# Moving the operand tiles of TensorE to other byte offsets in a hybrid decoder layer

## The chip, the cores and the metric

The kernel runs on one core of a Trainium2 chip. The metric is device time in microseconds of one execution. Four compute engines matter: TensorE (PE in the profile, with its weight loads as a row of their own, PEld), VectorE (DVE), ScalarE (ACT) and GpSimd (POOL). SyncE (SP) issues most of the transfers. A product on PE has a stationary operand of 128 rows by 128 columns, which a weight load brings into the array, and a moving operand of 128 rows by up to 512 columns that streams through it. Both are read from the on-chip memory (SBUF), where a tile occupies the same byte range in each of 128 partitions; an address below is a byte offset in a partition.

## The reference

One layer over 512 tokens of width 1024, all in float32: a norm, one wide input projection, two token mixers side by side, a gated merge with a residual, and an MLP with a residual and a last norm.

```python
h = rms_norm(x, norm_mix[l])
proj = h @ w_in[l]
u, q, kc, vc, ksl, vsl, kwn, vwn, g_nsa, g_merge = jnp.split(proj, IN_SPLITS, axis=-1)
y_pool = pool_mixer(u, w_pool[l], pool_scale[l])
y_nsa = nsa_mixer(q, kc, vc, ksl, vsl, kwn, vwn, g_nsa, ...)
g_a, g_b = jnp.split(jax.nn.sigmoid(g_merge), 2, axis=-1)
merged = g_a * (y_pool @ w_proj_pool[l]) + g_b * (y_nsa @ w_proj_nsa[l])
x = x + merged @ w_out[l]
h = rms_norm(x, norm_mlp[l])
x = x + jnp.square(jax.nn.relu(h @ w_ff1[l])) @ w_ff2[l]
return rms_norm(x, norm_final)
```

The pooling mixer takes causal means over windows of 2, 4, 8 and 16 tokens. The other mixer is attention with 16 heads of 64 over compressed keys, selected blocks and a window; with 512 tokens all blocks are selected and the window holds all tokens.

## The kernel before

Each float32 product is made of three products in the fp32r type: operand A is split into a high part AH and a low part AL, B likewise, and AH·BH, AH·BL and AL·BH are summed in PSUM (`split_products`). ScalarE makes the high part of a weight by a copy, VectorE the low part by a subtraction. So every operand of PE exists as a pair of tiles.

The work goes in stages, in the order of the program, which is written out by hand:

- Tokens are loaded, normed, turned and split into `hT = (R1, R2)`, two tiles of 128 partitions by 8 blocks by 512 tokens. (0 to about 30 us.)
- The input projection: for each key of the list `P1` the 128 columns of weights are loaded into one of four `raw` buffers, split into a slot `wh`, `wl` (two slots of each), and multiplied with `hT` by `fm`: 8 blocks by 3 products of 512 columns with the weights stationary. The first two keys and the second half of the gates (`Group`, keys with G) run at 256 columns instead.
- The attention loop: 96 steps, each with scores, exponentials, transposes and products with the values, and beside them as filler the keys of `FILL2`, again 512-column products of `hT` with `wh`, `wl`. Its result goes into `OT`, which is `hT` again.
- The projections `pn0` to `pn7` of `OT`, the merge, and `w_out`, partly by seven sums of 256 columns (`Out`), partly at 512 columns with resident tiles `mH`, `mL` and `W1H`, `W1L`.
- The MLP, four chunks. Both layers use Strassen-like sums of seven products for four. Layer 1 (`Group`) multiplies weights that stand still with token tiles of 256 columns: `x11`, `x21`, `x22`, `xT1` live in quarters of R1 and R2 (`Rf`, `XB`), `xT2`, `xT3`, `xT4` in the pool `a4`. Its results become `y` tiles (`YB`). Layer 2 of the first three chunks (`Wide`) holds the `y` tiles stationary and streams 512 columns of weights; the last chunk does it at 256 columns (`Out`) and the rest at 512 or 256 (`last_half`).

In the MLP and around it a weight goes into one of three slots in turn: two of `wh`, `wl` and one of `w3h`, `w3l`, which is put ahead in the list `slots_hl`. `product` and `Wide.pe` issue the products in the order that their loops give, and every 6 or 3 products the next step of a weight's preparation and of the side work.

Tiles come from pools. A pool lays its tiles one behind another in the order in which they are first asked for, each start rounded up to 32 bytes; pools stand behind each other in the order of opening, and a closed pool's room is used again. The pool `const` holds `ident`, `eps_t`, R1, R2, MA, `tick`, GB (also `scratch` and a tile `TS` of sums) and `identR`; behind it stand `weights` (`raw`, `wh`, `wl`), then the pools of the stages: `op` and `att` with `p0`, `p1`, `p2` in turn, later `p3` (x1, `sq`), `p4` (`w3h`, `w3l`, `raw5`, `junk`), and above them `q3` and, after it, `a4`.

Of the kernel before, what the change touches and what calls it, by code (L numbers as in the profile page):

```python
# [13 lines left out]
F32 = mybir.dt.float32  # L14
FR = mybir.dt.float32r
# [5 lines left out]
S = 512  # L21
# [4 lines left out]
NT = S // 128  # L26
# [36 lines left out]
def trunk(ctx: ExitStack, tc: tile.TileContext, A, out):  # L63
# [4 lines left out]
    def pool(name, **kw):  # L68
        return tc.tile_pool(name=name, bufs=1, reuse_waits="tile", **kw)
# [8 lines left out]
    cp = ctx.enter_context(pool("const"))  # L78
    wp = ctx.enter_context(pool("weights"))

    ident = cp.tile([128, 128], F32, name="ident")
    eps_t = cp.tile([128, 1], F32, name="eps_t")
    R1 = cp.tile([128, 8, S], FR, name="R1")
    R2 = cp.tile([128, 8, S], FR, name="R2")
    MA = cp.tile([128, 8, S], F32, name="MA")
    MAf = MA.rearrange("p j t -> p (j t)")

# [3 lines left out]
    def quarter(f, i):  # L91
        return f[:, 1024 * i:1024 * i + 1024].rearrange("p (k t) -> p k t", k=4)
# [510 lines left out]

    hT = (R1, R2)
    f_banks = [2]
# [43 lines left out]
    def bcast(v, n):  # L649
        return bass.AP(tensor=v.tensor, offset=v.offset, ap=[[0, 128], [1, n]])  # L650

    POOL.memset(eps_t, EPS)
    tick = cp.tile([128, 1], F32, name="tick")
    ACT.activation(tick, eps_t, AF.Sqrt)
    e2 = ExitStack()
    op = e2.enter_context(pool("op"))
# [190 lines left out]
    with ExitStack() as c1:  # L847
# [247 lines left out]
        for k in P1[2:]:  # L1095
            i = int(k[-1]) if k[-1].isdigit() else None
            if k[-2] == "G":
                if not gate_f:
                    t = p1.tile([128, 16, 128], FR, tag="cA", bufs=1, name="gs")
# [47 lines left out]
    with ExitStack() as c2:  # L1147
# [237 lines left out]
        n = len(slots)  # L1385
# [4 lines left out]
        for i in range(n + LAG + PLAG):  # L1390
            if i < n:
                p = slots[i][0]
# [9 lines left out]
            t = i - LAG  # L1402
# [19 lines left out]
            j = t - PLAG  # L1422
# [26 lines left out]
    p3 = ctx.enter_context(pool("p3"))  # L1449
    ps3 = ctx.enter_context(pool("ps3", space=PSUM))  # L1450
    XX = p3.tile([128, NT, D], F32, name="x1")
    X1 = [XX[:, t, :] for t in range(NT)]
    sq = p3.tile([128, NT, 8], F32, name="sq")

    def bank():
        return ps3.tile([128, S], F32, tag="B", bufs=8, name="psB")
# [8 lines left out]
    def tm3_resident(ws, aT, post):  # L1465

        for t in range(NT):
            ps = bank()
            prods = []
            for k in range(8):  # L1470
                wH, wL = ws[k // 2]
                prods += split_products(*aT(k, t), wH[:, k % 2, :], wL[:, k % 2, :])
            for _ in pieces(ps, prods, prepare=t > 0):
                step_side()
            post(t, ps)
# [6 lines left out]
    XQ = {b: quarter(MAf, i) for i, b in enumerate(("11", "12", "21", "22"))}  # L1482
    XT = quarter(GBf, 0)
    turned = [0]
    Rf = [R.rearrange("p j t -> p (j t)") for R in (R1, R2)]
    XB = {b: [quarter(f, i) for f in Rf] for i, b in enumerate(("11", "21", "22", "T1"))}
    slots_hl.insert(0, [p4.tile([128, 1024], FR, name=f"w3{e}") for e in "hl"])
    give_back(p4.tile([128, 1024], F32, name="raw5"))
# [119 lines left out]
    with ExitStack() as c3:  # L1608
        q3 = c3.enter_context(pool("q3"))
        gB = q3.tile([128, D], F32, name="gB1")  # L1610
        nc.sync.dma_start(gB, bcast(A["norm_mlp"][0], D))
        mT = (q3.tile([128, 8, S], FR, name="mH"), q3.tile([128, 8, S], FR, name="mL"))
        W1 = (q3.tile([128, 8, S], FR, name="W1H"), q3.tile([128, 8, S], FR, name="W1L"))
        keep([f"wo1{i}" for i in range(4)], W1)
# [13 lines left out]
        class Merged:  # L1628
# [4 lines left out]
            def of(self, y):  # L1633
                return self.made[y]
# [24 lines left out]
        for j in range(3, 8):  # L1659
# [10 lines left out]
            if j == 3:  # L1670
                x, y = (M.part(b, slice(0, 4)) for b in ("11", "12"))
# [71 lines left out]
            side.append(g)  # L1743
        tm3_resident(w1, mTs, post1)
    a4 = ctx.enter_context(pool("a4"))
    for b in ("T2", "T3", "T4"):
        XB[b] = [a4.tile([128, 4, 256], FR, name=f"x{b}{e}") for e in "HL"]

    YB = {b: [a4.tile([128, 4, 256], FR, name=f"y{b}{e}") for e in "HL"]
          for b in ("11", "21", "22", "T1", "T2", "T3", "T4")}  # L1750
    YF = {"11": quarter(GBf, 0), "12": quarter(GBf, 1), "21": quarter(GBf, 2), "22": quarter(MAf, 1)}

    def halves(x, f):
# [2 lines left out]
    class Hidden:  # L1756
# [10 lines left out]
        def of(self, b):  # L1767
            return XB["T2"] if b == "12" else YB[b]

# [188 lines left out]
```

## Time and profile before

| | |
|---|---|
| median of 3 runs | 792.78 us (792.71 to 793.98) |
| the profiled execution | 792.2 us, span 790.4 us |
| busy: PE, PEld | 774.8 us, 685.7 us |
| busy: DVE, ACT, POOL | 658.6 us, 504.6 us, 175.1 us |
| products | 4795 |
| granted clock | 0.999 |
| DMA | 140.80 MB, mean 178 GB/s |

The span is from the first to the last instruction of the program; the device time has a little before and after it. A row of a group of instructions has its line, engine, operation, the tile that it writes and those that it reads (buffer numbers left out, so R1 and R2 are both R, and `wh` is either of two slots), the shape and the count; behind the bar the time in which any of the group ran, the mean duration of one in ns, and the idle time before them. Products overlap: the next one starts before the one before has ended, so durations do not add up. The timeline has the start of each instruction and its duration in us; equal ones in succession are merged into one row with their count.

### The profile page before, as it was taken

How to read it: one execution, taken by the hardware profiler on the slowest of the kernel's cores; microseconds unless marked ns; L12 is line 12 of the kernel's file. 1: busy time of each engine (PE TensorE's matmuls, PEld its weight loads, DVE VectorE, ACT ScalarE, POOL GpSimd, SP SyncE). 2: the span in 40 equal slices, each digit the busy share in tenths (PEclk: the TensorE clock that was granted, in tenths of full speed). 3: DMA queues.
4: the chain of work that ended last, by engine and by line, in shares of the span. 5: the costliest groups of instructions: out<-in, count | busy, mean ns of one | idle time of the engine just before them, and what ended most of it. 6: DMA issues, size and time to landing. Idle time of an engine off the chain costs nothing. (4 is left out here: it accounts for less than half of the span.)

```text
span 790.4 us, 13452 instructions
## 1 busy us (share of the span) xinstructions
PE 774.8 (98%) x4795; PEld 685.7 (87%) x4795; DVE 658.6 (83%) x1274; ACT 504.6 (64%) x977; POOL 175.1 (22%) x257
## 2 busy tenths in 40 slices
PE   8999999999999999999999999999999999999996
PEld 6889889878878888888889899879987999799986
DVE  6999858557989988998689689997899789998974
ACT  6668536337978888899545576943783378347833
POOL 4000000015847766563000210101110110010001
PEclk9999999999999999999999999999999999999999
DMA  9453732474566731011667998979998999897622
GB/s 302 129 163 99 196 94 83 118 212 121 74 160 115 162 67 41 27 55 60 165 208 211 294 228 250 289 200 292 288 280 215 297 270 287 213 267 217 189 78 107
DMA packets 118013, 140.80 MB, mean 178 GB/s; under 512 B 5477, under 2 KB 94729, under 8 KB 117770
## 3 DMA queue, kind: packets, MB, share of 16 engines
q1 hardware_dynamic: 98026, 116.64, 45.8%
q0 software_dynamic: 19632, 22.55, 19.1%
q8 instruction: 38, 0.62, 0.3%
q10 hardware_dynamic: 288, 0.75, 0.3%
q14 instruction: 29, 0.24, 0.1%
HBM read 135.20 MB, written 47.19 MB: 231 GB/s over the span
## 5 line engine op out<-in xcount | busy, mean ns | idle before, releaser
L497 PE MATMUL psF<-R,wh 128*128 128x512 f32 x448 | 145.9, 403 | 0.8 <-ACT scratch L869 0.8
L349 ACT ACTIVATE wh<-raw 128x1024 fp32r<-128x1024 f32 x70 | 73.8, 1056 | 72.3 <-PE psB L567 28.5
L311 POOL DMA_DIRECT2D S<-w_ff x40 | 45.1, 1128 | 311.2 <-DMA S<-w_ff 202.9
L352 DVE TENSOR_TENSOR wl<-raw,wh 128x1024 fp32r<-128x1024 f32 x70 | 85.2, 1220 | 18.9 <-ACT wh L349 18.6
L1316 POOL TENSOR_SCALAR P<-P,sm,GT 128x128 f32<-128x128 f32 (+3 forms) x128 | 85.2, 684 | 69.8 <-DVE sm L1313 44.6
L497 PEld LDWEIGHTS psF<-R,wh 128*128 128x128 f32 x448 | 80.5, 188 | 15.8 <-ACT scratch L869 1.0
L497 PE MATMUL psF<-R,wl 128*128 128x512 f32 x224 | 89.1, 398 | 1.3 <-DVE wl L456 1.3
L454 ACT ACTIVATE wh<-raw 128x512 fp32r<-128x512 f32 (+1 forms) x84 | 49.9, 618 | 58.9 <-PE psF L497 31.0
L1303 ACT ACTIVATE P<-P,sm 128x128 f32<-128x128 f32 (+3 forms) x128 | 71.1, 557 | 8.8 <-DVE sm L1293 6.0
L456 DVE TENSOR_TENSOR wl<-raw,wh 128x512 fp32r<-128x512 f32 (+1 forms) x82 | 56.4, 702 | 22.6 <-ACT wh L454 22.2
L1293 DVE CUSTOM_DVE_ANT_0 P<-psS,cst 128x128 f32<-128x128 f32 (+3 forms) x128 | 59.4, 482 | 4.8 <-PE psT L1333 2.4
L567 PE MATMUL psB<-R,wh 128*128 128x256 f32 x336 | 60.8, 282 | 0.0
L1349 DVE TENSOR_TENSOR PT<-psT,PT 128x512 fp32r<-128x512 f32 (+2 forms) x96 | 56.2, 591 | 3.4 <-ACT PT L1344 3.0
L349 ACT ACTIVATE w3h<-raw 128x1024 fp32r<-128x1024 f32 x35 | 37.0, 1057 | 33.5 <-PE psB L567 14.3
L1344 ACT ACTIVATE PT<-psT 128x512 fp32r<-128x512 f32 (+2 forms) x96 | 49.2, 521 | 12.2 <-PE psT L1333 10.9
L567 PEld LDWEIGHTS psB<-R,wh 128*128 128x128 f32 x336 | 51.7, 189 | 0.4
L497 PEld LDWEIGHTS psF<-R,wl 128*128 128x128 f32 x224 | 42.1, 188 | 11.1 <-DVE wl L456 1.8
L1333 PE MATMUL psT<-ident,P 128*128 128x128 f32 x320 | 50.1, 272 | 0.2
L1367 PE MATMUL psO<-PT,VV 128*128 128x256 f32 x320 | 48.5, 286 | 0.0
L352 DVE TENSOR_TENSOR w3l<-raw,w3h 128x1024 fp32r<-128x1024 f32 x35 | 42.7, 1219 | 6.3 <-ACT w3h L349 6.2
L1333 PEld LDWEIGHTS psT<-ident,P 128*128 128x128 f32 x320 | 39.7, 140 | 8.8 <-issue 1.2
L567 PE MATMUL psB<-R,wl 128*128 128x256 f32 x168 | 47.2, 281 | 0.0
(487 smaller groups left out, 2215.2 us busy)
## 6 DMA issues: line engine op xcount, KB each, us to landing
raw<-w_ff SPq DMA_DIRECT2D x55, 512.0 KB, 6.9
S<-w_ff POOLq DMA_DIRECT2D x40, 512.0 KB, 8.6
raw<-S SPq DMA_DIRECT2D x40, 512.0 KB, 5.3
raw<-w_in SPq DMA_DIRECT2D x32, 512.0 KB, 4.1
S<-w_ff SPq DMA_DIRECT2D x30, 512.0 KB, 7.4
S<-S SPq DMA_DIRECT2D x10, 512.0 KB, 6.4
raw<-w_proj_nsa SPq DMA_DIRECT2D x8, 512.0 KB, 3.9
x<-x SPq DMA_DIRECT2D x7, 512.0 KB, 6.5
```

The costliest lines, as they stand in the source:

```text
L349: ACT.activation(h, t, AF.Copy)
L352: DVE.tensor_tensor(l, t, h.bitcast(F32), op=ALU.subtract)
L454: ACT.activation(h[:, sl], t[:, sl], AF.Copy)
L456: eng.tensor_tensor(l[:, sl], t[:, sl], h[:, sl].bitcast(F32), op=ALU.subtract)
L497: PE.matmul(ps, a, b, start=first and j == 0, stop=last and j == n - 1, skip_group_check=True)
L567: PE.matmul(out, w[u][:, k, 128 * f:128 * f + 128], moving[v][:, k, :], **kw)
L1293: DVE.tensor_tensor_reduce(out=P[:, o:o + n].rearrange("p (a c) -> p a c", c=128), in0=s, in1=m, scale=1.0, scalar=3e38, op0=ALU.add, op1= ...
L1303: last_exp[:] = [ACT.activation(c, c, AF.Exp, bias=sm[:, 0, e:e + 1], scale=-1.0, accum_out=sm[:, 1, e:e + 1])]
L1316: r = POOL.tensor_scalar(P[:, o:o + n], P[:, o:o + n], sm[:, 2, e:e + 1], GT[:, qb, c + e:c + e + 1], op0=ALU.mult, op1=ALU.mult)
L1333: PE.transpose(pt[:, 128 * j:128 * j + 128], P[:, 128 * j:128 * j + 128], ident)
L1344: ACT.activation(dH, src, AF.Copy)
L1349: return DVE.tensor_tensor(dL, src, dH.bitcast(F32), op=ALU.subtract)
```

## The change

The tiles get other addresses, by five edits; no instruction is added, removed or put elsewhere, apart from the operands' addresses.

- `tick` is asked for ahead of R1 instead of behind MA.
- R1 and R2 become 64 and 8 elements longer, and each has two views: the plain one, from element 0, in 8 blocks, for `hT` and `OT`; and a flat one from element 8 (32 bytes on), which takes the place of `Rf` in the quarters of the MLP and of `w_out`.
- An unused tile of 56 elements stands ahead of the weights' tiles, another ahead of `mH`.
- `sq` has 16 elements a token block instead of 8.
- In `a4` the `y` tiles come first, then an unused tile of 8 elements, then the `x` tiles.

```diff
--- before.py
+++ after.py
@@ -80,8 +80,16 @@
 
     ident = cp.tile([128, 128], F32, name="ident")
     eps_t = cp.tile([128, 1], F32, name="eps_t")
-    R1 = cp.tile([128, 8, S], FR, name="R1")
-    R2 = cp.tile([128, 8, S], FR, name="R2")
+    tick = cp.tile([128, 1], F32, name="tick")
+
+    def two_bases(name, n):
+
+        t = cp.tile([128, n], FR, name=name)
+        return t[:, 0:8 * S].rearrange("p (j t) -> p j t", j=8), t[:, 8:8 + 8 * S]
+
+    R1, R1f = two_bases("R1", 8 * S + 64)
+    R2, R2f = two_bases("R2", 8 * S + 8)
+    wp.tile([128, 56], F32, name="gap")
     MA = cp.tile([128, 8, S], F32, name="MA")
     MAf = MA.rearrange("p j t -> p (j t)")
 
@@ -650,7 +658,6 @@
         return bass.AP(tensor=v.tensor, offset=v.offset, ap=[[0, 128], [1, n]])
 
     POOL.memset(eps_t, EPS)
-    tick = cp.tile([128, 1], F32, name="tick")
     ACT.activation(tick, eps_t, AF.Sqrt)
     e2 = ExitStack()
     op = e2.enter_context(pool("op"))
@@ -1450,7 +1457,7 @@
     ps3 = ctx.enter_context(pool("ps3", space=PSUM))
     XX = p3.tile([128, NT, D], F32, name="x1")
     X1 = [XX[:, t, :] for t in range(NT)]
-    sq = p3.tile([128, NT, 8], F32, name="sq")
+    sq = p3.tile([128, NT, 16], F32, name="sq")
 
     def bank():
         return ps3.tile([128, S], F32, tag="B", bufs=8, name="psB")
@@ -1482,7 +1489,7 @@
     XQ = {b: quarter(MAf, i) for i, b in enumerate(("11", "12", "21", "22"))}
     XT = quarter(GBf, 0)
     turned = [0]
-    Rf = [R.rearrange("p j t -> p (j t)") for R in (R1, R2)]
+    Rf = (R1f, R2f)
     XB = {b: [quarter(f, i) for f in Rf] for i, b in enumerate(("11", "21", "22", "T1"))}
     slots_hl.insert(0, [p4.tile([128, 1024], FR, name=f"w3{e}") for e in "hl"])
     give_back(p4.tile([128, 1024], F32, name="raw5"))
@@ -1609,6 +1616,7 @@
         q3 = c3.enter_context(pool("q3"))
         gB = q3.tile([128, D], F32, name="gB1")
         nc.sync.dma_start(gB, bcast(A["norm_mlp"][0], D))
+        q3.tile([128, 56], F32, name="gap")
         mT = (q3.tile([128, 8, S], FR, name="mH"), q3.tile([128, 8, S], FR, name="mL"))
         W1 = (q3.tile([128, 8, S], FR, name="W1H"), q3.tile([128, 8, S], FR, name="W1L"))
         keep([f"wo1{i}" for i in range(4)], W1)
@@ -1743,11 +1751,11 @@
             side.append(g)
         tm3_resident(w1, mTs, post1)
     a4 = ctx.enter_context(pool("a4"))
+    YB = {b: [a4.tile([128, 4, 256], FR, name=f"y{b}{e}") for e in "HL"]
+          for b in ("11", "21", "22", "T1", "T2", "T3", "T4")}
+    a4.tile([128, 8], F32, name="gap")
     for b in ("T2", "T3", "T4"):
         XB[b] = [a4.tile([128, 4, 256], FR, name=f"x{b}{e}") for e in "HL"]
-
-    YB = {b: [a4.tile([128, 4, 256], FR, name=f"y{b}{e}") for e in "HL"]
-          for b in ("11", "21", "22", "T1", "T2", "T3", "T4")}
     YF = {"11": quarter(GBf, 0), "12": quarter(GBf, 1), "21": quarter(GBf, 2), "22": quarter(MAf, 1)}
 
     def halves(x, f):
```

## The prediction

> **What bounds the kernel now.** I read the page's first two parts, the table by stages, the waits, and then the products by form.
>
> ```profile
> span 790.4 us, 13452 instructions
> PE 774.8 (98%) x4795; PEld 685.7 (87%) x4795; DVE 658.6 (83%) x1274; ACT 504.6 (64%) x977; POOL 175.1 (22%) x257
> PEclk9999999999999999999999999999999999999999
> ...
> 40.00:180.00 140.00, 138.91 (x750) 119.34 (x749) 103.60 (x185) 71.84 (x125) 4.46 (x9) 1.00 0.50 135
> 240.00:370.00 130.00, 129.20 (x842) 113.93 (x840) 119.19 (x392) 112.91 (x303) 80.81 (x122) 1.00 0.29 63
> 440.00:500.00 60.00, 60.00 (x434) 56.43 (x434) 49.67 (x72) 41.51 (x73) 8.10 (x8) 1.00 0.98 252
> 500.00:580.00 80.00, 79.38 (x506) 71.14 (x505) 69.26 (x82) 47.79 (x65) 8.94 (x8) 1.00 0.96 264
> ...
> PE psF L497 <- DVE wl L456: 1.3, 1, 1.3
> ACT wh L349 <- PE psB L567: 28.5, 18, 1.8
> ACT wh L349 <- DMA raw<-w_ff: 4.0, 2, 2.5
> ```
>
> In a stage row the columns behind the length are PE, PEld, DVE, ACT and POOL busy, the granted clock, the DMA engines' share and GB/s. PE is busy for nearly all of every stage at full clock, and its longest single wait after the start is 1.3 us. In the MLP (from 440 us) ScalarE, which splits the weights, waits mostly for PE to free a slot (28.5 us in one group) and little for loads (4.0 us). So the time is the sum of the distances between the starts of successive products. A product's own duration overlaps the next one's; what counts is that distance, read from the timeline. But the duration of a form moves with it:
>
> ```profile
> L497 PE MATMUL psF<-R,wh 128*128 128x512 f32 x448 | 145.9, 403 | 0.8 <-ACT scratch L869 0.8
> L497 PE MATMUL psF<-R,wl 128*128 128x512 f32 x224 | 89.1, 398 | 1.3 <-DVE wl L456 1.3
> L497 PE MATMUL psB<-R,wh 128*128 128x512 f32 x80 | 25.1, 396 | 0.0
> L497 PE MATMUL psF<-yd,wh 128*128 128x512 f32 x64 | 19.8, 390 | 0.8 <-DVE MA L1133 0.8
> L497 PE MATMUL psB<-R,wl 128*128 128x512 f32 x40 | 15.8, 396 | 0.0
> L1577 PE MATMUL psB<-wh,y22H 128*128 128x512 f32 x16 | 6.3, 395 | 0.0
> L1577 PE MATMUL psB<-wl,y22H 128*128 128x512 f32 x16 | 6.3, 394 | 0.0
> L1577 PE MATMUL psB<-w3h,y22H 128*128 128x512 f32 x8 | 3.1, 390 | 0.0
> L1577 PE MATMUL psB<-w3l,y22H 128*128 128x512 f32 x8 | 3.1, 390 | 0.0
> ```
>
> The last four rows are one line, one shape and one stationary tile, in the same stage; only the weight slot differs, and products on slot w3 are 4 to 5 ns shorter. `yd` with `wh` is 390 too, `R` with `wh` 396 to 403.
>
> **Where the tiles lie.** Tiles are laid one behind another, each start rounded up to 32 bytes. In the program built from the kernel before, the bases modulo 256 are: R1, R2 160; wh, wl 192; w3h, w3l, mH, mL, W1, x and y tiles 64; yd 192; GB and the T sums in it 192. By hand for the change: R1 starts at 17,088 (remainder 192) because `tick` now lies ahead of it, R2 16,640 bytes on (192), the second views 32 bytes further (224), wh at 100,032 (192). `sq`, 128 bytes longer, puts w3 on 192; gap and order in a4 put y on 192 and x on 224; gap in q3 puts mH on 160; GB comes to 224. The tiles of the attention move by 512 bytes and keep their distances.
>
> Distance is moving minus stationary, modulo 256. The timeline gives the spacing of each from the starts of two groups:
>
> ```profile
> 141.59 0.62 PE L497 MATMUL psF<-R,wh 128*128 128x512 f32 x2
> 147.19 0.40 PE L497 MATMUL psF<-yd,wh 128*128 128x512 f32 x1
> ...
> 419.06 0.28 PE L1527 MATMUL psB<-wh,R 128*128 128x256 f32 x1
> 421.87 0.28 PE L1527 MATMUL psB<-w3h,R 128*128 128x256 f32 x1
> ...
> 437.72 0.40 PE L497 MATMUL psB<-W1H,mH 128*128 128x512 f32 x1
> 448.65 0.49 PE L1705 MATMUL psB<-ident,xs 128*128 128x128 f32 x3
> ...
> 490.48 0.28 PE L567 MATMUL psB<-xT4H,w3h 128*128 128x256 f32 x1
> 493.35 0.40 PE L567 MATMUL psB<-R,wh 128*128 128x256 f32 x2
> 496.19 0.28 PE L567 MATMUL psB<-xT4H,wh 128*128 128x256 f32 x1
> 499.03 0.40 PE L567 MATMUL psB<-R,w3h 128*128 128x256 f32 x2
> 501.91 0.39 PE L1577 MATMUL psB<-wh,y11H 128*128 128x512 f32 x1
> ...
> 536.42 0.40 PE L1577 MATMUL psB<-wh,y22H 128*128 128x512 f32 x1
> 542.01 0.40 PE L567 MATMUL psB<-R,w3h 128*128 128x256 f32 x2
> ```
>
> 512 columns: distance 224 (R at 141.59, 24 products) 5.60/24 = 233.3 ns; 128 (from 536.42, 24) 5.59/24 = 232.9; 0 (from 437.72, 48) 10.93/48 = 227.7. 256 columns, 24 each: distance 32 (from 419.06) 2.81/24 = 117.1; 0 (490.48) 2.87/24 = 119.6; 224 (493.35) and 128 (496.19) 2.84/24 = 118.3; 96 (499.03) 2.88/24 = 120.0. It is the distance and not a tile's own place: distance 0 is fast with both at 192 (yd) and with both at 64 (w3 and y), and 192 against 64 is slow.
>
> **The change part by part.** No instruction, wait or transfer is added or taken away. Per form, count by difference:
> - 512 columns. All R with wh, wl go from 224 to 0: 448 + 224 in psF, 80 + 40 in psB, 24 of the same form in psT (one key: 8 blocks by 3 products), 816 x 5.6 ns = 4.57 us. The wide products on wh, wl (7 sums by 3 products by 16) go from 128 to 0: 336 x 5.2 = 1.75. In the last half 60 products, from 96 to 0, spaced as the other slow ones by my estimate: 60 x 5.3 = 0.32. Sum 6.64 us.
> - 256 columns that come to 32: R with wh, wl in the MLP, 504 from 224, x 1.2 = 0.60; R with w3, 264 from 96, x 2.9 = 0.77; x tiles and mH with wh, wl, 456 from 128, x 1.2 = 0.55; x tiles with w3 and a part of the gates, 240 from 0, x 2.5 = 0.60. Sum 2.52.
> - 256 columns that lose: first keys and half the gates on the plain tokens, 168 from 224 to 0, x 1.3 = 0.22; last products on y, 120 from 128 to 0, 0.16; 48 of w_out from 32 to 224, 0.06. Sum 0.44.
> - 304-column and 128-column products change distances that I can't price: 96 + 64 products; bound by the spread of the rows, 3 ns either way, 0.5 us either way. I take nothing, the middle, and keep both ends.
>
> That is 8.7 us if PE sets the pace everywhere. In the attention it shares the pace: between 240 and 370 us VectorE is busy for 119.2 and ScalarE for 112.9 of 130 us. There the fillers number 181 + 91:
>
> ```profile
> L497 PE MATMUL psF<-R,wh 128*128 128x512 f32 x181 | 61.4, 412 | 0.0
> L497 PE MATMUL psF<-R,wl 128*128 128x512 f32 x91 | 36.4, 400 | 1.3 <-DVE wl L456 1.3
> ```
>
> 272 x 5.6 = 1.5 us stands between nothing and all; I take half and subtract 0.75. Left: 7.9 us.
>
> Costs that I set to nothing. The longer tiles: no transfer or evacuation grows. ScalarE and VectorE at other addresses: the split of a weight takes 1056 ns into wh at 192 and 1057 into w3h at 64:
>
> ```profile
> L349 ACT ACTIVATE wh<-raw 128x1024 fp32r<-128x1024 f32 x70 | 73.8, 1056 | 72.3 <-PE psB L567 28.5
> L349 ACT ACTIVATE w3h<-raw 128x1024 fp32r<-128x1024 f32 x35 | 37.0, 1057 | 33.5 <-PE psB L567 14.3
> 413.61 1.06 ACT L1653 ACTIVATE R<-GB 128x1024 fp32r<-128x1024 f32 x1
> 416.23 1.06 ACT L402 ACTIVATE wh<-raw 128x1024 fp32r<-128x1024 f32 x1 [1.55 <-PE psB L497]
> ```
>
> A quarter of the second view reaches 8 elements into the next plain block. So the split of T1 at 413.61, which writes blocks 2 and 3 of R during the last projection, must also await block 4: 3 products, 0.7 us. Behind it on ScalarE is the `wh` of 416.23, which idles 1.55 us anyway; that covers it. Late f2 loads into the plain view await x tiles that were read long before.
>
> A rule speaks against all this. The Trainium skill, TensorE: Matmul & The Clock Gate, Step-by-step: what each phase is for, says that the moving operand and the weight load have independent read ports, so that loading the next weights doesn't steal read bandwidth from the running product. By it no distance matters and the sum is nothing, against 8.7 us by the rows; the trace (390 against 394 and 395) does not agree.
>
> **The rivals.**
> 1. The MLP is paced by loads once PE is faster. For it: the DMA engines' share of 0.98 and 0.96 from 440 to 580. Against it: ScalarE waits 28.5 us for PE in one group and 4.0 for loads. Of the sum, 504 x 1.2, 264 x 2.9, 384 x 1.2, 192 x 2.5 and 336 x 5.2 lie there, 4.1 us; without them 7.9 - 4.1 = 3.8 us are left: 788.4 on the profile, 789.0 as median.
> 2. Nothing happens: a product and the weight load beside it don't meet in the memory, and the slot, or the order of its use, makes the difference between the rows, not its address; or a gap tile that nothing uses gets no bytes. For it: wh and w3 differ in more than address. Against it: yd with wh is fast. The sum is 0, 792.8. (The rule of the Trainium skill above, on TensorE: Matmul & The Clock Gate, gives this one.)
> 3. Slower: the 256-column products do badly at 32. 1,464 of them go there, for which I have one place where 24 products stand alone (117.1). The rest of the sum is 6.64 - 0.44 - 0.75 = 5.45 us. To end 1.6 us slower they must cost 7.05/1464 = 4.8 ns more than their 118.8 now, so from 123.6 ns on; at 125 ns it is 9.1 - 5.45 = 3.6 us slower, 796.4. No quoted row is above 120.0.
> 4. All is realised, attention too, and the unpriced products help by 0.5: 792.2 - 9.2 = 783.0, as median 783.6.
>
> **How the numbers follow.** The profiled execution took 792.2 us (span 790.4), the runs 792.71 to 793.98 with median 792.78, 0.6 above it. 792.2 - 7.9 = 784.3, as median 784.9. Chances: this 0.62, rival 1 0.20, rival 2 0.09, rival 3 0.04, rival 4 0.05. The range 783.2 to 789.5 holds the forecast and rival 1, with some of rival 4. The likeliest case alone has 783.6 to 786.5: the attention's share whole or lost, and the unpriced 0.5 lost. 0.2% (1.6 us) is about what a measurement of this kernel can tell from none: faster 0.87, within 0.09, slower 0.04.
>
> **What would show it.** Durations of R with wh or wl at 512 columns outside the attention at 390 instead of 396; wh and w3 alike at 390 in the wide products; 24 x products of 256 columns in 2.81 us; the stages from 40 to 180 and from 440 on shorter by 2 and 4 us. Against it: new waits of ScalarE for `raw` (rival 1), durations unchanged (2), 256-column groups above 2.97 us (3).

## The result and the profile after

The kernel after takes 786.13 us as median of 4 runs, beside 792.75 us for the kernel before in the same session: a ratio of 0.991, 95% interval [0.9896, 0.9923]. One of the 4 runs took 1079.53 us at a granted clock of 0.657; the median counts it, the ratio does not, and the other three took 785.54 to 786.53 us. A repetition with 5 rounds gave 786.33 us (785.32 to 787.94) beside 793.4, ratio 0.9917 [0.9904, 0.9929]. The forecast was 784.9 us, in a range of 783.2 to 789.5; the likeliest case alone had 783.6 to 786.5. So the gain is 6.6 to 7.1 us, by the two medians and ratios, where 7.9 were forecast. The profiled execution took 786.53 us. Its page, first lines (the lines of the kernel after stand 7 or 8 further down: L505 was L497, L575 was L567, L1584 was L1577):

```profile
span 784.8 us, 13451 instructions
PE 766.2 (98%) x4795; PEld 681.7 (87%) x4795; DVE 659.1 (84%) x1274; ACT 505.0 (64%) x977; POOL 175.2 (22%) x257
```

PE is busy for 8.6 us less, with the same 4795 products; the other engines' busy times stay within 0.5 us. The products by form:

```profile
L505 PE MATMUL psF<-R,wh 128*128 128x512 f32 x448 | 144.3, 399 | 0.7 <-ACT scratch L876 0.7
L575 PE MATMUL psB<-R,wh 128*128 128x256 f32 x336 | 60.0, 279 | 0.0
L505 PE MATMUL psB<-R,wh 128*128 128x512 f32 x80 | 24.6, 389 | 0.0
L1584 PE MATMUL psB<-wh,y22H 128*128 128x512 f32 x16 | 6.2, 389 | 0.0
L1584 PE MATMUL psB<-w3h,y22H 128*128 128x512 f32 x8 | 3.1, 389 | 0.0
```

`R` with `wh` outside the attention has come from 396 to 389 ns, and `wh` and `w3h` in the wide products, 395 and 390 before, are now both 389. The first row, which holds the attention's fillers too, has only come from 403 to 399.

Durations overlap, so the time is read from the starts. First some rows of the timeline of before that the prediction did not need, then the timeline of after; the first number is the start in us.

```profile
226.72 0.40 PE L497 MATMUL psF<-R,wl 128*128 128x512 f32 x1
365.64 0.71 PE L497 MATMUL psF<-R,wh 128*128 128x512 f32 x2
366.88 0.40 PE L497 MATMUL psF<-R,wl 128*128 128x512 f32 x1
```

```profile
140.16 0.40 PE L505 MATMUL psF<-R,wh 128*128 128x512 f32 x1
145.62 0.62 PE L505 MATMUL psF<-yd,wh 128*128 128x512 f32 x2
224.82 0.39 PE L505 MATMUL psF<-R,wl 128*128 128x512 f32 x1
363.69 0.71 PE L505 MATMUL psF<-R,wh 128*128 128x512 f32 x2
364.94 0.40 PE L505 MATMUL psF<-R,wl 128*128 128x512 f32 x1
487.25 0.28 PE L575 MATMUL psB<-xT4H,w3h 128*128 128x256 f32 x1
490.05 0.39 PE L575 MATMUL psB<-R,wh 128*128 128x256 f32 x2
492.85 0.28 PE L575 MATMUL psB<-xT4H,wh 128*128 128x256 f32 x1
495.65 0.39 PE L575 MATMUL psB<-R,w3h 128*128 128x256 f32 x2
498.45 0.39 PE L1584 MATMUL psB<-wh,y11H 128*128 128x512 f32 x1
533.71 0.39 PE L1584 MATMUL psB<-wh,y22H 128*128 128x512 f32 x1
539.15 0.40 PE L575 MATMUL psB<-R,w3h 128*128 128x256 f32 x2
```

24 products of `R` at 512 columns take 145.62 - 140.16 = 5.46 us, 227.5 ns each (233.3 before). The four stretches from 487.25 to 498.45 take 2.80 us each, 116.7 ns a product; before they took 2.87, 2.84, 2.84 and 2.88. The lead of the kernel after is the difference of the starts of one product in the two traces: 1.43 us at the `R` product of 140.16, 1.90 at 224.82, 1.95 at 363.69, 3.23 at 487.25, 3.46 at 498.45, 2.71 at 533.71, 2.86 at 539.15, and 5.6 at the end of the span. So the stretch from 224.82 to 363.69, inside the attention, gave 0.05 us; and at the first wide products 0.75 us was lost again.

What took the place of the missing part is in PE's waits at the wide products and at `w_out` (total in us, times, longest), of before and then of after:

```profile
PE psB L1577 <- DVE wl L352: 0.6, 1, 0.6
PE psB L1577 <- ACT wh L349: 0.2, 1, 0.2
PE psB L1577 <- ACT w3h L349: 0.2, 1, 0.2
```

```profile
PE psB L1584 <- DVE wl L360: 1.4, 2, 0.9
PE psB L1584 <- ACT w3h L357: 0.5, 1, 0.5
PE psB L1584 <- ACT wh L357: 0.5, 1, 0.5
PE psB L1534 <- ACT R L1661: 0.4, 1, 0.4
```

The three waits at the wide products, 1.0 us before, have become 2.4 us, and that for `R` at `w_out` is new in the list. In the repetition's execution the four are 0.8, 0.5, 0.5 and 0.4: how much is lost there differs between executions.

For the account I matched the products of two traces one by one, took the distances from the programs' addresses, and summed the change of each start-to-start interval; intervals that moved by more than 60 ns are stalls and stand apart. The spacings, means without stalls: 512 columns from 224 or 128 to 0 outside the attention, 232.9 to 227.4 ns; 256 columns to 32, from 118.3 (224), 118.5 (128), 119.8 (96) and 119.6 (0) to 116.7 or 116.8.

| intervals, us against the trace of before | first execution | repetition |
|---|---|---|
| 512 columns, moved, before and between attention and MLP | -2.9 | -3.0 |
| 512 columns, moved, in the attention | -0.3 | -0.3 |
| 512 columns, moved, in the MLP | -2.2 | -2.3 |
| 256 columns, moved (gains and losers) | -2.7 | -2.8 |
| stalls, first 40 us | +1.1 | +0.3 |
| stalls, 40 to 440 us | +0.6 | +0.6 |
| stalls, MLP | +2.0 | +0.8 |
| all others | +0.1 | 0.0 |
| sum | -4.4 | -6.7 |

The first execution starts its first product 1.2 us earlier in the span than the one of before (it waits 2.3 us for `grow` there, not 3.5) and gives that back in the first 40 us, so -4.4 and -1.2 make its 5.6 us of span; the repetition's span is 783.5 us, 6.9 below 790.4. The moved products give 8.1 us in the one and 8.4 in the other; 6.6 to 7.1 of it reach the time.

### The profile page after: what moved, and what is told of

It reads as the page before. It is cut to its first block, busy times and chain, and to the rows that moved or that the text cites. A ratio compares the mean times of both kernels' runs of the same rounds, so it can differ in the third digit from the quotient of the medians.

```text
span 784.8 us, 13451 instructions
## 1 busy us (share of the span) xinstructions
PE 766.2 (98%) x4795; PEld 681.7 (87%) x4795; DVE 659.1 (84%) x1274; ACT 505.0 (64%) x977; POOL 175.2 (22%) x257
## 5 line engine op out<-in xcount | busy, mean ns | idle before, releaser
L505 PE MATMUL psF<-R,wh 128*128 128x512 f32 x448 | 144.3, 399 | 0.7 <-ACT scratch L876 0.7
L505 PEld LDWEIGHTS psF<-R,wh 128*128 128x128 f32 x448 | 80.5, 188 | 14.5 <-ACT scratch L876 0.9
L505 PE MATMUL psF<-R,wl 128*128 128x512 f32 x224 | 88.4, 394 | 1.3 <-DVE wl L464 1.3
L575 PE MATMUL psB<-R,wh 128*128 128x256 f32 x336 | 60.0, 279 | 0.0
L575 PEld LDWEIGHTS psB<-R,wh 128*128 128x128 f32 x336 | 51.4, 188 | 0.2
L505 PEld LDWEIGHTS psF<-R,wl 128*128 128x128 f32 x224 | 42.0, 188 | 10.4 <-DVE wl L464 1.7
L575 PE MATMUL psB<-R,wl 128*128 128x256 f32 x168 | 46.9, 279 | 0.0
```

The costliest lines, as they stand in the source:

```text
L505: PE.matmul(ps, a, b, start=first and j == 0, stop=last and j == n - 1, skip_group_check=True)
L575: PE.matmul(out, w[u][:, k, 128 * f:128 * f + 128], moving[v][:, k, :], **kw)
```

## The experiments

**Once more.** The kernel after, unchanged, in more rounds (786.33 us, above), as the reference for the others of its session.

> The changed kernel once more, beside the three kernels below on one chip. Expected ratio to the kernel before 0.991 to 0.992, some 786 us; the stages from 40 to 180 us and from 440 us on carry the gain, the attention between 200 and 360 us nothing.

**The wide products undone.** Only the 816 products of `R` at 512 columns go back to a distance of 224; the quarters keep theirs.

```diff
-    tick = cp.tile([128, 1], F32, name="tick")
+    tick = wp.tile([128, 1], F32, name="tick")
-        ... t[:, 8:8 + 8 * S]
+        ... t[:, 16:16 + 8 * S]
-    R2, R2f = two_bases("R2", 8 * S + 8)
-    wp.tile([128, 56], F32, name="gap")
+    R2, R2f = two_bases("R2", 8 * S + 16)
+    wp.tile([128, 48], F32, name="gap")
```

> The plain view of R1 and R2 goes back to distance 224 from wh and wl, and the flat view stays at 32, so the 816 products of 512 columns with R are undone and the rest of the change stays. Theory (the distance sets the spacing, and PE does not set the pace in the attention): their spacing goes back from about 227.5 to 233 ns; the 544 products outside the attention cost 544 x 5.5 = 3.0 us, the 168 narrow ones on the plain view give 0.2 back: about 2.8 us slower than the changed kernel, ratio near 0.995. Rival (half or all of the attention's 272 counts too): 3.5 to 4.3 us, ratio 0.9955 to 0.9965. Rival (not the distance): no difference from the changed kernel.

789.27 us, ratio 0.9954 [0.9941, 0.9966]: 2.9 us of the gain gone. From the groups by form and the timeline of this kernel:

```profile
L505 PE MATMUL psF<-R,wh 128*128 128x512 f32 x448 | 146.0, 403 | 0.8 <-ACT scratch L876 0.8
```

```profile
141.39 0.39 PE L505 MATMUL psF<-R,wh 128*128 128x512 f32 x1
146.99 0.40 PE L505 MATMUL psF<-yd,wh 128*128 128x512 f32 x1
```

24 products are back at 5.60 us. The rise lies at 40 to 200 us (1.4) and 360 to 440 us (1.1); between them, in the attention, it is 0.1 to 0.2.

**The narrow products undone.** The wide ones stay at 0. The flat view starts at element 0 and the plain one at 8, and the gap in `a4` goes: `R` in the MLP comes to 224 and the `x` tiles to 0.

```diff
-    tick = cp.tile([128, 1], F32, name="tick")
+    tick = wp.tile([128, 1], F32, name="tick")
...
-        return t[:, 0:8 * S].rearrange(...), t[:, 8:8 + 8 * S]
+        return t[:, 8:8 + 8 * S].rearrange(...), t[:, 0:8 * S]
...
-    a4.tile([128, 8], F32, name="gap")
```

> Here the products of 512 columns keep distance 0, but those of 256 columns lose the 32: 768 with R in the MLP go to 224, 576 with the x tiles to 0. Theory: spacing 118.3 and 119.6 ns instead of 116.75: 768 x 1.55 + 576 x 2.85 = 2.8 us slower than the changed kernel, ratio near 0.995. Rival (the narrow products' gain is lost to waits anyway): under 1 us slower.

789.43 us, ratio 0.9947 [0.9934, 0.9961]: 3.1 us of the gain gone. The spacings of 623 products rose from 116.7 to 119.5 and of 768 from 116.7 to 118.4 ns, 3.0 us by their counts. By the ratios to the kernel before, the two halves are worth 2.9 and 2.4 us. The 336 wide products on `y` in the MLP, which went from 128 to 0, are undone in neither kernel; by their spacings (232.9 and 227.4 ns) they hold another 1.8 us. The three parts come to more than the 6.6 to 7.1 us of the whole, which fits waits that grow when PE gets faster. The groups by form show the two groups apart:

```profile
L575 PE MATMUL psB<-R,wh 128*128 128x256 f32 x336 | 60.9, 282 | 0.1
L575 PE MATMUL psB<-xT4H,wh 128*128 128x256 f32 x40 | 11.4, 284 | 0.4 <-DVE MA L596 0.4
```

**The overlap of the second view.** The sums for `w_out` are written into the plain view, so that T1's split no longer reaches into block 4.

```diff
+    Rp = [R.rearrange("p j t -> p (j t)") for R in (R1, R2)]
...
-            h, l = (quarter(f, n) for f in Rf)
+            h, l = (quarter(f, n) for f in Rp)
```

> The sums T1 to T4 ahead of w_out are written into the plain view instead of the flat one, so the split of T1 need not await block 4 of the last projection. Theory (the overlap of the two views delays the splits and makes the wait of some 0.4 us at 419 us in the changed kernel): that wait goes back to the 0.1 us of before; 96 products go from 224 to 0 and cost 96 x 1.2 = 0.1 us: 0.2 to 0.4 us faster than the changed kernel. Rival (the wait comes from elsewhere): 0.1 us slower, and the wait stays.

786.62 us, ratio 0.9919 [0.9905, 0.9932], the same as the reference, so that neither expectation came whole. The wait on `R` at L1661 (from the start of one product to the next it was 331 ns before and 721 after) is gone, but PE then waits 0.4 us for `MA` in its place, and 96 products of `w_out` move from 118.4 to 119.7 ns:

```profile
PE psB L1535 <- ACT MA L1549: 0.4, 1, 0.4
```

The overlap costs nothing that shows in the time.

**Does PE pace the attention?** The attention gave nothing, and VectorE and ScalarE are busy for 118.9 and 113.6 of 130 us there. Two theories: they set the pace, or PE does and its spacing did not fall. This kernel leaves the last two products out of each sum of 24 of the fillers, 26 in all.

```diff
-        yield from pieces(ps, fm_products(wH, wL, xT, sub, nk))
+        prods = fm_products(wH, wL, xT, sub, nk)
+        yield from pieces(ps, prods[:-2] if mode["pool"] else prods)
```

> The changed kernel without the last two of 24 products in each of the 13 fillers of the attention (the low parts of one block are left out), 26 x 228 = 5.9 us less of PE's work there. Theory (ScalarE and VectorE set the pace in the attention): at most 1.5 us shorter than the changed kernel. Rival (PE sets it, and the shorter spacing was lost for another reason): 4 to 6 us shorter.

780.47 us, ratio 0.9847 [0.9831, 0.9863]: 5.9 us below the reference by the medians and 5.5 by the ratios (the two ran on different chips), nearly as much as 26 products of 228 ns. In the traces, from the first `KH,Q` product to the last `PT,VV`, the kernel after takes 193.7 us and this one 188.8; 22 of the 26 products lie there, 22 x 228 = 5.0 us. PE paces the attention. The spacing is what did not fall: in the rows above, the five intervals of one filler group of six take 366.88 - 365.64 = 1.24 us before and 364.94 - 363.69 = 1.25 us after. In the 28 groups of six the mean intervals were 315.9, 232.0, 231.4, 233.3, 231.6 and 266.4 ns before, and are 315.5, 231.1, 233.0, 232.1, 227.1 and 267.7 after: the fast spacing shows in the fifth alone.

**The wide products' waits.** The square of the activations, which ScalarE computes beside the weight splits, is left out.

```diff
-            ACT.activation(r, r, AF.Square)
```

> The changed kernel without the square after the relu in the MLP (left out), 0.52 us of ScalarE each, 32 in all; no product, load or split of weights changes. Theory (at the start of the wide products ScalarE and VectorE, busy with the y tiles, split the next weights too late, and PE waits there): PE's waits in the wide products, 0.9, 0.5 and 0.5 us and more at 507 to 510 and 668, shrink by at least half, 1.5 to 2.5 us shorter than the changed kernel. Rival (the loads come too late): the waits stay, under 0.7 us shorter.

784.62 us, ratio 0.9893 [0.9876, 0.9909]: 1.7 us below the reference by the medians, 1.9 by the ratios, with intervals that overlap, so that the gain in time is not clear of noise. The waits at the wide products:

```profile
PE psB L1584 <- DVE wl L360: 0.6, 1, 0.6
PE psB L1584 <- ACT w3h L357: 0.2, 1, 0.2
PE psB L1584 <- ACT wh L357: 0.2, 1, 0.2
```

They are 1.0 us as before, in place of 2.4 in the first execution and 1.8 in the repetition, with 0.2 us for `yT3L` beside them. Two of the stalls tell most: from the start of `w3l,yT3H` near 594 and of `wl,yT3H` near 673 us to the next product it took 617 and 626 ns before, 892 and 898 (in the repetition 881 and 881) after, and 631 and 632 without the square. With the narrow products undone, when PE comes there later, they were 789 and 793. So the square, or VectorE's sums that wait for it, accounts for the growth of those two; which of the two it is was not parted. The stalls at the first wide products (504 to 513 us) differ in place and size in each of the three executions, and the whole difference of 1.7 us is more than these waits hold; where the rest of it lies was not settled.

**Streams alone.** 48 products of 512 columns and 72 of 256 at each distance, with nothing on the other engines but a copy of 8 columns by ScalarE behind each stream; nothing of the layer is computed.

```python
def stream(name, n, pairs, count):
    for i in range(count):
        m, s = pairs[i % len(pairs)]
        a, b = n * (i % (4096 // n)) + m // 4, 128 * (i % 31) + s // 4
        PE.matmul(ps[:, 0:n], T[:, b:b + 128], M[:, a:a + n], ...)
```

> Streams of products alone, with no other work beside them: two tiles with one base modulo 256, each product with the next 128 columns as weights; 48 products of 512 columns and 72 of 256 for each distance of moving minus stationary. The output is a copy of weights and of a few sums, nothing of the layer is computed. Theory (distance modulo 256): 512 columns 227 ns at 0 and 233 at the others; 256 columns 116.8 at 32, 118.3 at 128 and 224, 119.6 at 0, 120 at 96. Both operands shifted by 96 (the stream shift) as at 0. Two more streams change the address from product to product: in own each product's two operands are 0 apart and the weights that are loaded beside it, for the next product, 128 away from what it streams; in next it is the other way round. If a product collides with the load of the next weights, own is slow (233) and next fast (227); if its own operands matter, the reverse. Rival (the spacings came from the other engines' work): all distances alike.

The timeline has one row for a stream (its name has the columns and the distance), so the difference of two starts is the time of 48 or 72 products:

```profile
29.96 11.04 PE L50 MATMUL n512d0x<-M,T 128*128 128x512 f32 x48
40.84 11.28 PE L50 MATMUL n512d16x<-M,T 128*128 128x512 f32 x48
...
130.20 11.35 PE L50 MATMUL n512d224x<-M,T 128*128 128x512 f32 x48
141.39 11.14 PE L50 MATMUL n512ownx<-M,T 128*128 128x512 f32 x48
...
185.24 8.80 PE L50 MATMUL n256d0x<-M,T 128*128 128x256 f32 x72
193.87 8.71 PE L50 MATMUL n256d16x<-M,T 128*128 128x256 f32 x72
202.42 8.56 PE L50 MATMUL n256d32x<-M,T 128*128 128x256 f32 x72
210.82 8.68 PE L50 MATMUL n256d48x<-M,T 128*128 128x256 f32 x72
219.34 8.32 PE L50 MATMUL n256d64x<-M,T 128*128 128x256 f32 x72
227.50 8.80 PE L50 MATMUL n256d96x<-M,T 128*128 128x256 f32 x72
```

512 columns: 10.88/48 = 226.7 ns at 0 and 11.19/48 = 233.1 at 224. 256 columns: 119.9 at 0, 116.7 at 32, 113.3 at 64. The layer's spacings are reproduced without any other engine, with one more tempting value: 64. Both tiles moved together by 96 bytes kept 227.1 and 120.0. Streams of 512 columns that alternated between two places, so that a product's own distance was 0 and that to the next weights 128, or the other way round, came to 228.7 and 230.0, neither fast nor slow: which of the two distances counts stays open.

**A finer scan and short groups.** 17 distances, and groups of 6 products of 512 columns parted by 4 of 128, as in the attention.

> Streams of products alone; nothing of the layer is computed, so its time stands beside no other kernel's. 48 products of 512 columns and 72 of 256 columns at each of the distances 0, 4, 8, 52, 56, 60, 64, 68, 72, 76, 80, 112, 176, 208, 240, 256 and 320 bytes (moving minus stationary tile), then, at distances 0, 64 and 224, 16 groups of 6 products of 512 columns with 4 products of 128 columns behind each group. Theory (the spacing is set by the distance modulo 256): 256 repeats 0 (226.7 ns and 120.0 ns), 320 repeats 64 (229.0 and 113.3); the good places are narrow, so that 52 and 76 are back at 232 or more for 512 columns and 117 or more for 256. Second theory (it goes by a larger unit than 256 bytes, or by the absolute place): 256 and 320 differ from 0 and 64 by over 2 ns. For the short groups: if the distance of 0 shortens each product alike, the groups at 0 are 6 x 6.3 = 38 ns shorter than those at 224; if it needs a long unbroken stream, as the attention stage of the changed kernel suggests, the difference is under 15 ns.

```profile
363.37 29.28 PE L64 MATMUL short0x<-M,T 128*128 128x512 f32 x160
392.48 29.49 PE L64 MATMUL short64x<-M,T 128*128 128x512 f32 x160
```

The places are narrow: at 512 columns 4 bytes off, the spacing is 235.8 instead of 226.7 ns. 256 repeats 0 (226.7 and 119.8 ns), as the theory asks, and so does 320 repeat 64 at 512 columns (229.3 and 229.1). But at 256 columns it does not: 117.8 instead of 113.3 ns. The short groups took 29.11/16 = 1.82 us at a distance of 0 and 1.84 at 224. Both expectations missed (38 ns, or under 15): in a group at 0 the spacings were 284, 232, 231, 227, 226 and 227 ns, at 224 they were 287, 231, 230, 230, 235 and 231, so the first products run at the slow spacing and only the later ones at the fast one.

**Narrow products at 64.** The kernel after with its 256-column products at 64 instead of 32 bytes.

```diff
+    both = cp.tile([128, 2], F32, name="eps_t")
+    eps_t, tick = both[:, 0:1], both[:, 1:2]
-        ... t[:, 8:8 + 8 * S]
+        ... t[:, 16:16 + 8 * S]
-    a4.tile([128, 8], F32, name="gap")
+    a4.tile([128, 16], F32, name="gap")
```

(with R2 eight elements longer and the gaps ahead of the weights and of `mH` at 48)

> The changed kernel with its 256-column products at a distance of 64 rather than 32 bytes, the 512-column ones still at 0. Theory: the spacing of the 256-column products falls from 116.75 to 113.3 ns as in the streams alone; 1464 of them x 3.4 = 5.0 us less of TensorE's work, of which 2 to 5 us reach the time, the rest being taken by waits for weight preparation on ScalarE and VectorE and for loads: 781 to 784 us, ratio to the kernel before 0.985 to 0.989. Rival (narrow products inside the layer do not follow the streams alone, or the preparation of the weights now sets the pace of the MLP): 785.5 to 787, ratio 0.991.

787.84 us, ratio 0.9934 [0.9918, 0.995]; both expectations missed, on the slow side. One stretch of 24 products in its timeline:

```profile
488.59 0.28 PE L575 MATMUL psB<-xT4H,w3h 128*128 128x256 f32 x1
491.42 0.28 PE L575 MATMUL psB<-R,wh 128*128 128x256 f32 x1
```

2.83/24 = 117.9 ns, not 113.3. So the rival was right that narrow products in the layer do not follow the streams alone, but its time was too short. Over all 1463 the mean is 117.6 instead of 116.8, 1.2 us more; two waits for `xs` near 452 and 462 us add 1.3 us in this execution, and other stalls are shorter by about as much. The ratio's interval overlaps that of the reference. Oddly, the 120 products of `w_out` that this edit took from 224 to 192 ran at 114.2 ns instead of 118.3, a distance that gave 117.8 alone. So for 256 columns the distance does not fix the spacing.

**What else fixes it?** Streams at 32, 64, 192 and 320, with both tiles shifted, or with one product of another width ahead.

> Streams alone again (nothing of the layer is computed): 72 products of 256 columns at distances 32, 64, 192 and 320 bytes, each with both tiles shifted together by 0, 32, 96 or 128 bytes, or with one product of 64, 128, 304 or 512 columns ahead of the stream, or with the moving block held fixed; and 32 products of 512 columns at distance 0 with the same shifts and openings. First theory (the distance modulo 256 alone sets the spacing): each distance has one spacing, 64 and 320 the same one. Second theory (a stream settles into one of several steady patterns, and what runs ahead of it decides which): at 64, 192 or 320 the spacing jumps between about 113.5 and about 117.8 ns with the opening product or the shift, at equal distance. Third theory (the absolute place decides): it changes with the shift and not with the opening product. At 512 columns and distance 0 all theories expect 226.7 to 227.4 for every opening.

Timeline at 192: the number behind `s` is the shift of both tiles, that behind `b` the columns of the opening product.

```profile
181.98 8.34 PE L50 MATMUL n256d192s0x<-M,T 128*128 128x256 f32 x72
190.15 8.65 PE L50 MATMUL n256d192s32x<-M,T 128*128 128x256 f32 x72
198.63 8.64 PE L50 MATMUL n256d192s96x<-M,T 128*128 128x256 f32 x72
...
232.31 8.33 PE L50 MATMUL n256d192b304x<-M,T 128*128 128x256 f32 x72
240.48 0.39 PE L46 MATMUL n256d192b512x<-M,T 128*128 128x512 f32 x1
240.71 8.64 PE L50 MATMUL n256d192b512x<-M,T 128*128 128x256 f32 x72
249.19 0.99 PE L50 MATMUL n256d192fixedx<-M,T 128*128 128x256 f32 x7
```

113.5 ns without a shift and 117.8 with 32; 113.5 behind a product of 304 columns and 117.8 behind one of 512, at the same addresses. At 64, where it had been 113.3 twice, all nine streams now ran at 117.8 (the three kernels of streams ran on three chips). At 32 the openings gave 116.7 or 117.8. At 512 columns and distance 0 all seven settled at 227, after up to ten uneven spacings (224 to 236) at the start. The first theory falls, since one distance has two spacings, and the third, since streams at the same addresses differ: a stream of 256 columns has more than one steady pattern at one distance. That the opening product selects it, as the second theory says, is not shown, for each stream ran only once. The layer speaks for the moment rather than the order: two stretches of 24 products of `mH` with `wh`, `wl`, at a distance of 32, ran at 117.8 ns in the first execution of the kernel after and at 116.6 in its repetition, with the same program and the same addresses. What the choice follows was not settled.

## Why the prediction was right, and where its sum was off

- **PE's spacings set the time: right.** Undoing either half costs its own part, and removing 26 products saves nearly 26 spacings, even in the attention.
- **The distance, not the slot: right.** `wh` and `w3h` are alike at 389 ns. Rival 2 (nothing happens) falls: moving tiles changes the spacing by 6 ns in 233, also with PE running alone. With it falls what the prediction drew from the Trainium skill's rule of independent read ports (TensorE: Matmul & The Clock Gate, Step-by-step: what each phase is for), that no distance matters. Which weight load it is that a product meets stays open.
- **Wide products: right in sum.** 6.64 less 0.75 for the attention, 5.9, was forecast; 5.4 to 5.6 was measured. Outside the attention 5.1 was forecast and 5.1 to 5.3 came (232.9 to 227.4 ns each).
- **The attention: mis-sized, for a wrong reason.** Half of 1.5 us was taken because VectorE and ScalarE share the pace there. They do not, as the shortened fillers show. Only 0.3 us came. The fillers come mostly in groups of six or fewer, and the first products of a group run at the slow spacing. That explains about half of the loss: alone, a group of six still gains 20 of the 38 ns, in the layer some 4. Why the fast spacing comes still later there was not settled.
- **Narrow products: 2.52 - 0.44 = 2.1 forecast, 2.7 to 2.8 measured**, since they run at 116.7 rather than 117.1 ns and left 118.3 to 119.8. Rival 3 (32 is bad) falls.
- **Left out: the stalls.** The sum took all of PE's saving as time. PE arrives earlier at the start of the wide products, where the next weight's split was already late by 1.0 us in three waits; those grew by 0.8 to 1.4 us. Rival 1 had such waits with the loads as cause. Two of the stalls are shown to hang on the square and what follows it, and not on loads. One near 741 us, at `yT1L`, has a `raw` load of 4.36 us far back in its chain (725.86 us) and ScalarE's work between; it took 581 ns in the first execution, 155 in the repetition and 175 before, so it cannot be put down to the change. ScalarE's waits for `raw<-w_ff` in the MLP, the sign named for rival 1, came to 7.6 us before, 6.9 in the first execution and 10.6 in the repetition, which is the faster of the two. So rival 1 is not shown, and if it is there it is small.
- **"No instruction, wait or transfer is added or taken away": not quite.** The overlap of the second view put `wl<-raw,wh` ahead of the merge's second addition on VectorE and moved a few more instructions there and on ScalarE; with the overlap undone both orders are those of before. One instruction of waiting on VectorE fell away (13451), with the overlap or without. The delay at T1 that was said to be covered reached PE, 0.4 us at T1's first product, though undoing it gave no time back.
- **The signs named: most came.** The durations came to 389 ns where 390 was forecast, and 24 narrow products to 2.80 us where 2.81 was. The stretch from 40 to 180 us gave 1.5 us in both executions, not 2; that from 440 us on gave 3.0 and 4.4, not 4.
- **Together:** 8.7 - 0.75 = 7.9 was forecast; the spacings gave 8.1 to 8.4, the stalls took 1.7 of it back in the repetition, 6.6 to 7.1 is left. The likeliest case held with its own range of 783.6 to 786.5, in part by luck: the narrow products gave 0.6 us more than worked out, which made up for the 0.45 us that the attention lacked, and of the stalls the sum had nothing.

## What to carry to other kernels

Where TensorE sets the pace and a trace shows one product form with two durations, compare the byte distances of the operands before looking for waits; tile gaps of a few dozen bytes moved 0.8% of a kernel here. Take the spacing from long unbroken streams of the kernel itself, not from an isolated stream: a value that looked best alone (64 bytes at 256 columns) was no better in the layer. And when an engine that sets the pace gets faster, look up each place where it waits a little already: those waits grow first.

## What the runs showed of the hardware

- Spacing of fp32r products depends on the distance of moving and stationary tile to the granularity of 4 bytes: at 512 columns, with PE alone, 226.7 ns at 0 and 256, 229.1 at 64, 235.8 at 4, 239.4 at 68.
- At 256 columns one distance has several steady spacings (113.3 or 117.8 ns at 64 and at 192; 116.7 or 117.8 at 32, where the same products of one program took the one in one execution and the other in the next); at 512 columns and distance 0 there was one.
- A stream needs some products to reach the fast spacing: 284, 232, 231, then 227 ns in a short group, and up to ten uneven ones (224 to 236 ns) at the start of a long stream.
